# Block sums of the down projection's weights: made in attention with two tiles instead of beside the SSD with six

## The chip, the core and the metric

The kernel runs on one core of one Trainium2 chip. The metric is the device time of one execution in microseconds (us); the time of a kernel is the median of several runs. The engines of the core work side by side, each through its own list of instructions in order: TensorE (PE in the profile, with its weight loads as PEld), VectorE (DVE), ScalarE (ACT), GpSimd (POOL), and SyncE (SP), which here issues nearly all DMAs. Tiles lie in SBUF, matmul results in PSUM.

## What is computed

One decoder block over 1024 tokens of 1024 channels: a Mamba-2 SSD and a differential attention side by side, merged by gates, then a gated convolutional FFN. Cut to what matters here:

```python
h = rms_norm(x, pre_norm1_w[layer]) * (1.0 + sc1) + sh1
z, xbc, dt_raw, q, k, v, gates = jnp.split(h @ w_in[layer], IN_SPLITS, axis=-1)
y_ssd = ssd_branch(z, xbc, dt_raw, ...)
y_att = diff_attention_branch(q, k, v, ...)      # softmax 1 minus lam times softmax 2, per head
merged = gate_ssd * (y_ssd @ w_ssd_o[layer]) + gate_att * (y_att @ w_attn_o[layer])
x = x + g1 * rms_norm(merged @ w_out[layer], post_norm1_w[layer])
h2 = rms_norm(x, pre_norm2_w[layer]) * (1.0 + sc2) + sh2
u = causal_dwconv(h2 @ w_up[layer], conv_ffn_w[layer], conv_ffn_b[layer])
f = (jax.nn.gelu(u_gate, approximate=True) * u_val) @ w_down[layer]
x = x + g2 * rms_norm(f, post_norm2_w[layer])
```

## The kernel before

Every large matmul is split by hand: each operand is held as a rounded high part and a low part (the remainder), and three products replace one. On top of that, the up and the down projection use Strassen's scheme (in Winograd's form) on two by two blocks: seven block products instead of eight, for which sums and differences of the blocks of the weights are needed.

For the down projection these are the *block sums* of this document. `w_down` is 2816 x 1024. Its rows are taken as two halves of eleven groups (`KF` = 11) of 128 rows, its columns as two halves of 512, so group k has four blocks b11, b12, b21, b22 of 128 x 512. Needed are t1 = b12 - b11, t2 = b22 - t1, t3 = b22 - b12 and t4 = b21 - t2. They do not depend on the input, are made early in the kernel, written to the DRAM tensors `wtd["12"]` and `wtd["34"]`, and read back in the down projection at the end (`right_part`, L2161).

The kernel goes through these stages, by their place in the profiled execution (us from the start of its span): the norm and the projections of x up to 1147; the **SSD** from 1147 to 1744; the q and k projections' first blocks and the SSD's output projection up to about 2270; **attention** from about 2270 to 3300; the attention's output projection, `w_out`, the up projection from about 3640 to 4900, and the down projection.

*The SSD* (L1186 to L1242) goes through 16 units u, each half of a chunk of 128 tokens. In a unit are called, in the order in which they are written: `chunk_in(u+1)` (transposes and small products, the scaled input `xd` on DVE, `xdd` on GpSimd), `fill(2)`, `chunk_decay(u+1)` (decay matrices `M`, on ScalarE), `chunk_mask(u+1)` on DVE, `chunk_out(u)` (products `po` and `py`, then `tt` and `yt` on DVE), and `chunk_state(u)` (product `pst`, then `prev` on DVE). `fill(n)` emits n steps of the projection that makes the values v, six matmuls with 512 columns for two steps, which keeps TensorE at work. `run_bg(n)` runs n small pieces of a queue of background work, here mostly the chunk's norm. The list of engines given to `manual_schedule` (L1186: TensorE, VectorE, ScalarE, SP) says whose order is the one written; an engine that is not named is ordered by a planner with its own estimates. `sum_dn(u, n)` (L1180) is called at four places in a unit (L1212, L1215, L1223, L1227) and takes the next piece of `all_sums`, one subtraction of 128 x 512 on DVE. Sums are made in units 0 to 11, except unit 7 and half of unit 8. Six tiles of 512 KB serve them: four (`wdr`) for the blocks of two groups, which are loaded two groups ahead, and two (`wds`) for results, which are stored two by two.

*Attention* (L1592 to L1658) goes through 64 items t = (head j, block i of 128 queries). While item t is finished, the scores of t+1 are made. In the order of the code: `scores(t+1)` puts the score products on TensorE and behind them the transposes of item t's probabilities; then, on DVE, the mask (L1465 or L1475) and the row maxima (L1466 or L1476). `fill` emits steps of a stream of projections (three matmuls with 512 columns each), about four steps in an item. `probs(t+1)` has the exponentials on ScalarE (L1478, L1486, L1489), and on DVE the reciprocal (L1492), a coefficient (L1493) and the combination of the two softmaxes `p` (L1494). Then come `values(t)` on TensorE and at the end the bookkeeping. Background pieces are taken at four places in an item, two of them between the exponentials and the reciprocal. An item with i below 4 has up to 512 keys and uses one score buffer of two; one with i of 4 or more uses both. `load_heads` (L1425) loads the next head's queries, keys and values after item i = 3 (4 for the first head). The manual list here (L1592) is TensorE, VectorE, ScalarE and GpSimd, so SP's order comes from the planner.

Tiles of 512 KB come from `Slots` (L36), a pool of 43 with a first-in, first-out free list: what is freed first is taken first.

Of the kernel before, what the change touches and what calls it, by code (L numbers as in the profile page):

```python
# [11 lines left out]
F32 = mybir.dt.float32  # L12
F32R = mybir.dt.float32r
AF = mybir.ActivationFunctionType
ALU = mybir.AluOpType
AX = mybir.AxisListType

P = 128
D = 1024
S = 1024  # L20
HALF = 512
# [41 lines left out]
def kernel(ctx: ExitStack, tc: tile.TileContext, a: dict, out: bass.AP, dbg=None):  # L63
    nc = tc.nc
    V, A, G, T, SP = nc.vector, nc.scalar, nc.gpsimd, nc.tensor, nc.sync
# [6 lines left out]
    SL = Slots(sp, NSLOT)  # L72
# [331 lines left out]
    b12 = [hT[k][1] for k in range(KH)]  # L404
# [22 lines left out]
    KF = NFF // 2  # L427
    gld = {n: dp.tile([P, KF, HALF], F32, tag=f"gld_{n}", name=f"gld_{n}") for n in ("a11", "a12", "a22")}
    gld |= {n: dp.tile([P, KF, 2, HALF], F32, tag=f"gld_{n}", name=f"gld_{n}") for n in ("s12", "s34")}
    wtd = {n: dp.tile([P, KF, 2, HALF], F32, tag=f"wtd_{n}", name=f"wtd_{n}") for n in ("12", "34")}  # L430
# [170 lines left out]
    with tc.manual_schedule(engines={EN.PE, EN.DVE, EN.Activation, EN.SP}):  # L601
# [97 lines left out]
        for m, (kind, *_) in enumerate(pairs):  # L699
            last = m == len(pairs) - 1  # L700
            cg, cv = cgv[m % 2]
            x_, z_ = (0, 2) if m % 2 else (1, 3)
# [75 lines left out]

    dn_ops = deque()

    def down_load(k):
        if k < KF:
            for i in range(2):
                r0 = (k + KF * i) * P
                SP.dma_start(wdr[k % 2][i].rearrange("p h c -> p (h c)"), a["w_down"][r0 : r0 + P, :])

    def down_sums(k):
        (b11, b12), (b21, b22) = [(t[:, 0, :], t[:, 1, :]) for t in wdr[k % 2]]
        t1, t2, t3, t4 = wds[0][:, 0, :], wds[0][:, 1, :], wds[1][:, 0, :], wds[1][:, 1, :]
        V.tensor_tensor(t1, b12, b11, op=ALU.subtract)  # L790
        yield
        V.tensor_tensor(t2, b22, t1, op=ALU.subtract)
        SP.dma_start(wtd["12"][:, k, :, :], wds[0])
        yield
        V.tensor_tensor(t3, b22, b12, op=ALU.subtract)
        yield
        V.tensor_tensor(t4, b21, t2, op=ALU.subtract)
        SP.dma_start(wtd["34"][:, k, :, :], wds[1])
        down_load(k + 2)
        yield  # L800

    def all_sums():
        for k in range(KF):
            yield from down_sums(k)


    sm1 = SL.get("sm1", F32, (P, 8, 8, NH))
# [14 lines left out]
    f = lambda t: t.rearrange("p c h -> p (c h)")  # L822
# [350 lines left out]
            SP.dma_start(seq_w[n].rearrange("p k c -> p (k c)"), a[kind][b])  # L1173

    load_z(0)
    wdr = [[SL.get(f"wdr{i}{j}", F32, (P, 2, HALF)) for j in range(2)] for i in range(2)]
    wds = [SL.get(f"wds{i}", F32, (P, 2, HALF)) for i in range(2)]
    sums_dn = all_sums()

    def sum_dn(u, n):  # L1180
        if u == 7 or (u == 8 and n < 2):
            return
        for _ in range(2 if u < 2 and n == 3 else 1):
            next(sums_dn, None)

    with tc.manual_schedule(engines={EN.PE, EN.DVE, EN.Activation, EN.SP}):  # L1186
        for k in range(2):
            down_load(k)
        chunk_in(0)
        fill(2)  # L1190
        chunk_decay(0)
        chunk_mask(0, 0)
        chunk_mask(0, 1)
        lamt = const("lamt", [P, 2, 64])
        lams = const("lams", [P, 2])
        nlam = const("nlam", [P, 1])
        rl = rows[:, R_LAM : R_LAM + 256].rearrange("p (a b d) -> p a b d", a=2, b=2)
        V.tensor_tensor(lamt, rl[:, :, 0, :], rl[:, :, 1, :], op=ALU.mult)
        V.reduce_sum(lams, lamt, axis=AX.X)
        A.activation(lams, lams, AF.Exp)  # L1200
        V.tensor_tensor(nlam, lams[:, 1:2], lams[:, 0:1], op=ALU.subtract)
        V.tensor_scalar(nlam, nlam, -LAM_INIT, None, op0=ALU.add)
        subw = const("subw", [P, 1])
        V.tensor_scalar(subw, vec[:, V_SUB : V_SUB + 1], 1.0 - LAM_INIT, None, op0=ALU.mult)
        fill(4)
        for u in range(16):
            nxt = u + 1 < 16
            if nxt:
                chunk_in(u + 1)
            fill(2)  # L1210
            run_bg(2)
            sum_dn(u, 0)  # L1212
            if nxt:
                chunk_decay(u + 1)
            run_bg(1)  # L1215
            sum_dn(u, 1)
            if nxt:
                chunk_mask(u + 1, 0)
            fill(2)
            chunk_out(u, (lambda: chunk_mask(u + 1, 1)) if nxt else (lambda: None))  # L1220
            fill(3)
            run_bg(3)
            sum_dn(u, 2)  # L1223
            chunk_state(u)
            fill(1 if u % 3 else 0)
            run_bg(1)
            sum_dn(u, 3)  # L1227
            if u % 2 == 1:
                chunk_norm(u // 2)
            if u == 11:  # L1230
                assert next(sums_dn, None) is None
                SL.put(*wdr[0], *wdr[1], *wds)
                yr = [SL.get(f"yr{i}") for i in range(4)]
                ropc, rops = SL.get("ropc"), SL.get("rops")
                SP.dma_start(ropc, a["ropc"])
                SP.dma_start(rops, a["rops"])
                fetch_seq(0)
                fetch_seq(1)
            elif u == 12:
                load_y(0)  # L1240
        fill(16 * KD)
        run_bg(len(bg))  # L1242
# [345 lines left out]
    nfill = sum(2 * KD for _ in blocks) - NFIRST - NLAST  # L1588
    share = [4, 4, 4, 3, 4, 4, 4, 4]
    load_heads(0)  # L1590
    done = 0
    with tc.manual_schedule(engines={EN.PE, EN.DVE, EN.Activation, EN.Pool}):  # L1592
        for _ in range(NFIRST - 6):
# [5 lines left out]
        for t, (j, i) in enumerate(items):  # L1599
            quota = (j * sum(share) + sum(share[: i + 1])) * nfill // (8 * sum(share)) - done  # L1600
            done += quota
            quota += 2 if t == len(items) - 2 else 0
            f1 = quota // 2
            nxt = t + 1 < len(items)
            x = {}

            def first_turn():
                x[0] = transposes(t, 0)

            if nxt:  # L1610
                sc = scores(t + 1, first_turn)
            else:
                first_turn()
            fill(f1)
            f2 = (quota - f1 + 1) // 2
            if i >= 4:
                x[4] = transposes(t, 4)
            if nxt:
                probs(t + 1, sc, 2)
            run_bg(1)  # L1620
            values(t, 0, *x[0])
            fill(f2)
            if i % 4 == 2 and pend is not None:
                out_o(*pend)
            if i >= 4:
                values(t, 4, *x[4])
            fill(quota - f1 - f2)
            run_bg(1)
            emitted["values"] += 1
            if t == 55:  # L1630
                SL.put(*thl[0], *thl[1], *qst[0], *kst[0], *klo[0], vt[0])
                stg = [SL.get(f"stg{i}", F32, (P, 2, HALF)) for i in range(2)]
                for _ in range(4):
                    att_in()
            elif t > 56:
                for _ in range(2 if i % 2 else 1):
                    if n_att < 10:
                        att_split()
            if j < 7 and i == (4 if j == 0 else 3):
                load_heads(j + 1)  # L1640
            if i % 4 == 3:
                norm_o(j, i // 4)
                pend = (j, i // 4)
            elif i % 4 == 2:
                pend = None
# [775 lines left out]
```

## Time and profile before

| | us |
|---|---|
| timed runs | 1841.74, 1842.9, 1843.09 |
| median of the timed runs | 1842.9 |
| profiled execution, span from its first to its last instruction | 5463.1 |
| TensorE busy in the profiled execution | 5447.4 |
| VectorE busy | 1312.2 |
| ScalarE busy | 898.9 |
| GpSimd busy | 139.0 |

The profiled execution has no time of its own beside its span. The span is three times as long as a timed run; durations that are taken from the profile must be read with that in mind, TensorE's above all.

The profile lists for each engine how long it was busy, groups of instructions by line of the code (a group's row: line, engine, operation, output<-inputs, shapes, count | busy us, mean ns of one | idle time of the engine ahead of them and what ended it), the waits of one engine for another, the DMAs, and a timeline. In a row of stretches stand, for each engine, the busy us and, after it in brackets, the number of instructions.

### The profile page before, as it was taken

What the parts mean: (1) busy time and instruction counts of PE and PEld (TensorE: products, weight loads), DVE (VectorE), ACT (ScalarE), POOL (GpSimd) and SP (SyncE); (2) the same over time, 40 slices, a digit from 0 to 9 for tenths busy, and PEclk for the clock granted to TensorE, in tenths of its full rate; (3) what the DMA queues carried; (4) which work ended last, traced back from release to release, by engine and by line L of the source; (5) the groups of instructions that cost most, each with busy time, mean ns of one, the idle gap of its engine ahead of it and who ended that gap; (6) DMA issues with size and microseconds to landing.
All of it is one profiled execution on the core that took longest, in us unless ns stands there. A gap on an engine that the chain in (4) does not pass through costs nothing.

```text
span 5463.1 us, 24362 instructions
## 1 busy us (share of the span) xinstructions
PE 5447.4 (100%) x8922; PEld 3303.6 (60%) x8922; DVE 1312.2 (24%) x1984; ACT 898.9 (16%) x1744; POOL 139.0 (3%) x128
## 2 busy tenths in 40 slices
PE   9999999999999999999999999999999999999999
PEld 4555557766665555566677776556555555555555
DVE  4122222222221200022222231212333333332211
ACT  3111110011111100011122221102212111121210
POOL 0000000001110000000000000000000000000000
DMA  4021012212111212121122112210011111123221
GB/s 165 31 77 46 29 35 72 70 64 100 64 67 46 54 35 81 35 52 47 48 72 69 56 47 95 81 46 31 31 44 39 44 35 41 40 71 116 87 63 60
DMA packets 131368, 326.22 MB, mean 60 GB/s; under 512 B 14881, under 2 KB 39089, under 8 KB 131250
## 3 DMA queue, kind: packets, MB, share of 16 engines
q1 hardware_dynamic: 130290, 321.53, 18.2%
q0 software_dynamic: 960, 3.15, 0.2%
q8 instruction: 70, 1.15, 0.1%
q14 instruction: 48, 0.39, 0.0%
HBM read 229.45 MB, written 95.17 MB: 59 GB/s over the span
## 4 chain that ended last, share of the span: by engine, by line
PE 100%; issue 0%; ACT 0%; POOL 0%; DVE 0%; DMA 0%; DVEq 0%; POOLq 0%; ACTq 0%
PE upx L1822 4%; PE upx L1823 4%; PE upx L1821 4%; PE o L1515 4%; PE v L1028 2%; PE z L116 2%; PE v L1029 2%; PE z L118 2%; PE z L117 2%; PE xx L534 2%; PE so L117 2%; PE so L118 2%; PE xx L532 2%; PE upy L1821 2%; PE upy L1822 2%; PE upy L1823 2%
## 5 line engine op out<-in xcount | busy, mean ns | idle before, releaser
L1515 PEld LDWEIGHTS o<-vt,aT 128*128 128x128 f32 x576 | 201.1, 415 | 39.5 <-issue 33.8
L1821 PE MATMUL upx<-t,wu_t 128*128 128x512 f32 x264 | 218.9, 829 | 0.0
L1823 PE MATMUL upx<-t,wu_t 128*128 128x512 f32 x264 | 218.7, 828 | 0.0
L1822 PE MATMUL upx<-t,wu_t 128*128 128x512 f32 x264 | 218.7, 828 | 0.0
L1515 PE MATMUL o<-vt,aT 128*128 128x128 f32 x576 | 214.2, 578 | 0.0
L1456 PE MATMUL sc<-kst,qst 128*128 128x512 f32 (+2 forms) x192 | 141.7, 742 | 0.0
L1457 PE MATMUL sc<-klo,qst 128*128 128x512 f32 (+2 forms) x192 | 141.4, 746 | 0.0
L118 PE MATMUL so<-yT,w_ssd_o_lo 128*128 128x512 f32 x128 | 140.8, 1100 | 0.0
L117 PE MATMUL so<-yT,w_ssd_o_hi 128*128 128x512 f32 x128 | 140.8, 1100 | 0.0
L116 PE MATMUL so<-yT,w_ssd_o_hi 128*128 128x512 f32 x128 | 139.3, 1088 | 0.0
L1503 ACT COPY aT<-at 128x512 f32<-128x512 f32 (+2 forms) x96 | 45.9, 479 | 562.2 <-PE at L1502 562.2
L1822 PEld LDWEIGHTS upx<-t,wu_t 128*128 128x128 f32 x264 | 93.5, 354 | 63.8 <-issue 63.8
L1821 PEld LDWEIGHTS upx<-t,wu_t 128*128 128x128 f32 x264 | 93.4, 354 | 63.7 <-issue 62.7
L1823 PEld LDWEIGHTS upx<-t,wu_t 128*128 128x128 f32 x264 | 92.3, 350 | 63.8 <-issue 63.8
L1114 PEld LDWEIGHTS py<-xd,M 128*128 128x128 f32 x256 | 107.1, 596 | 34.8 <-issue 34.8
L1028 PE MATMUL v<-wv_hi,hT 128*128 128x512 f32 x96 | 121.5, 1266 | 0.0
L116 PE MATMUL z<-wz_hi,hT 128*128 128x346 f32 (+1 forms) x144 | 121.1, 841 | 0.0
L118 PE MATMUL z<-wz_hi,hT 128*128 128x346 f32 (+1 forms) x144 | 119.7, 832 | 0.0
L117 PE MATMUL z<-wz_lo,hT 128*128 128x346 f32 (+1 forms) x144 | 119.1, 827 | 0.0
L1502 PE MATMUL at<-ident,p 128*128 128x128 f32 x288 | 117.1, 576 | 0.0
L2184 PE MATMUL dx<-wdt_hi,g_hi 128*128 128x512 f32 x132 | 109.5, 830 | 0.0
L2186 PE MATMUL dx<-wdt_hi,g_lo 128*128 128x512 f32 x132 | 109.2, 827 | 0.0
(553 smaller groups left out, 10212.8 us busy)
## 6 DMA issues: line engine op xcount, KB each, us to landing
adas<-in_w_ada SPq DMA_DIRECT2D x32, 512.0 KB, 3.9
wdr<-in_w_down SPq DMA_DIRECT2D x22, 512.0 KB, 5.5
wtd<-wds SPq DMA_DIRECT2D x22, 512.0 KB, 2.9
wuf<-in_w_up SPq DMA_DIRECT2D x22, 512.0 KB, 3.5
gld_s<-gsum SPq DMA_DIRECT2D x22, 512.0 KB, 2.6
gst<-gld_s SPq DMA_DIRECT2D x20, 512.0 KB, 4.3
wdt_raw<-wtd SPq DMA_DIRECT2D x20, 512.0 KB, 3.9
wuv<-in_w_up SPq DMA_DIRECT2D x19, 512.0 KB, 3.6
```

The costliest lines, as they stand in the source:

```text
L116: T.matmul(ps, lh, rh, start=(i == 0), stop=False)
L117: T.matmul(ps, lh, rl, start=False, stop=False)
L118: T.matmul(ps, ll, rh, start=False, stop=(i == n - 1))
L1028: T.matmul(ps, xh_, wh, start=(k == 0), stop=False)
L1456: T.matmul(sc[:, n0:n1], qs_[s][:, tsl], ks_[s][:, n0:n1], start=True, stop=False)
L1457: T.matmul(sc[:, n0:n1], qs_[s][:, tsl], kl[s][:, n0:n1], start=False, stop=True)
L1502: T.transpose(ptr[:, k * P : (k + 1) * P], pt_[i % 2][0][:, (k0 + k) * P : (k0 + k + 1) * P], ident)
L1515: T.matmul(po_of[j, grp][:, qi, :], at[:, k, :], vt[j % 2][:, kt, :], start=(kt == 0), stop=(kt == i))
L1821: T.matmul(out_, wh, xh_, start=(k == 0 and first), stop=False, skip_group_check=not first)
L1822: T.matmul(out_, wh, xl_, start=False, stop=False, skip_group_check=not first)
L1823: T.matmul(out_, wl, xh_, start=False, stop=(k == end), skip_group_check=not first)
L2184: T.matmul(o, gh[:, kk, tsl], wh, start=(k == 0 and not more), stop=False, skip_group_check=more)
```

## The change

The same 44 subtractions are made, on the same engine. In the SSD all of them go, with their loads, their stores and the six tiles. In attention two tiles are taken, `wdr[0]` for b11 and b12 and `wdr[1]` for b21 and b22. A group takes five items: in the first four, one subtraction each, in place, in this order: b11 becomes t1 = b12 - b11, b12 becomes t3 = b22 - b12, b22 becomes t2 = b22 - t1, b21 becomes t4 = b21 - t2. Each result is stored at once, as 256 KB, and each tile is loaded for the next group behind the subtraction after which nothing needs its blocks any more: `wdr[0]` in the third item, `wdr[1]` in the fourth. The fifth item has none. Eleven groups in five items each make the items t = 0 to 54. The subtraction stands at the end of an item, ahead of the next item's scores and mask. After item 55 the tiles are freed with those of the attention.

```diff
-    def down_load(k):
+    def down_load(k, i):
         if k < KF:
-            for i in range(2):
-                r0 = (k + KF * i) * P
-                SP.dma_start(wdr[k % 2][i].rearrange("p h c -> p (h c)"), a["w_down"][r0 : r0 + P, :])
-
-    def down_sums(k):
-        (b11, b12), (b21, b22) = [(t[:, 0, :], t[:, 1, :]) for t in wdr[k % 2]]
-        t1, t2, t3, t4 = wds[0][:, 0, :], wds[0][:, 1, :], wds[1][:, 0, :], wds[1][:, 1, :]
-        V.tensor_tensor(t1, b12, b11, op=ALU.subtract)
-        yield
-        V.tensor_tensor(t2, b22, t1, op=ALU.subtract)
-        SP.dma_start(wtd["12"][:, k, :, :], wds[0])
-        yield
-        V.tensor_tensor(t3, b22, b12, op=ALU.subtract)
-        yield
-        V.tensor_tensor(t4, b21, t2, op=ALU.subtract)
-        SP.dma_start(wtd["34"][:, k, :, :], wds[1])
-        down_load(k + 2)
-        yield
+            r0 = (k + KF * i) * P
+            SP.dma_start(wdr[i].rearrange("p h c -> p (h c)"), a["w_down"][r0 : r0 + P, :])
 
     def all_sums():
+        (b11, b12), (b21, b22) = [(t[:, 0, :], t[:, 1, :]) for t in wdr]
         for k in range(KF):
-            yield from down_sums(k)
+            for n, (o, x_, y_) in enumerate(((b11, b12, b11), (b12, b22, b12), (b22, b22, b11), (b21, b21, b22))):
+                V.tensor_tensor(o, x_, y_, op=ALU.subtract)
+                SP.dma_start(wtd[("12", "34", "12", "34")[n]][:, k, n // 2, :], o)
+                if n > 1:
+                    down_load(k + 1, n - 2)
+                yield
+            yield
...
-    wdr = [[SL.get(f"wdr{i}{j}", F32, (P, 2, HALF)) for j in range(2)] for i in range(2)]
-    wds = [SL.get(f"wds{i}", F32, (P, 2, HALF)) for i in range(2)]
-    sums_dn = all_sums()
...
-            sum_dn(u, 0)
...
-            sum_dn(u, 1)
...
-            sum_dn(u, 2)
...
-            sum_dn(u, 3)
...
     load_heads(0)
+    wdr = [SL.get(f"wdr{i}", F32, (P, 2, HALF)) for i in range(2)]
+    sums_dn = all_sums()
+    for i in range(2):
+        down_load(0, i)
...
             emitted["values"] += 1
+            if t < 55:
+                next(sums_dn, None)
             if t == 55:
+                assert next(sums_dn, None) is None
+                SL.put(*wdr)
```

More of the change, by code (lines that the diff above doesn't have):

```diff
@@ L1175 @@
     load_z(0)
-    wdr = [[SL.get(f"wdr{i}{j}", F32, (P, 2, HALF)) for j in range(2)] for i in range(2)]
-    wds = [SL.get(f"wds{i}", F32, (P, 2, HALF)) for i in range(2)]
-    sums_dn = all_sums()
[L1180 to L1184, printed above, removed]
     with tc.manual_schedule(engines={EN.PE, EN.DVE, EN.Activation, EN.SP}):
-        for k in range(2):
-            down_load(k)
         chunk_in(0)
@@ L1230 @@
             if u == 11:
-                assert next(sums_dn, None) is None
-                SL.put(*wdr[0], *wdr[1], *wds)
                 yr = [SL.get(f"yr{i}") for i in range(4)]
```

## The prediction

> **What bounds the kernel now.** I read the head of the page first, because it says which engine fills the span.
>
> ```profile
> span 5463.1 us, 24362 instructions
> PE 5447.4 (100%) x8922; PEld 3303.6 (60%) x8922; DVE 1312.2 (24%) x1984; ACT 898.9 (16%) x1744; POOL 139.0 (3%) x128
> ```
>
> TensorE fills the profiled execution, but that execution lasted 5463.1 us and the timed ones 1842.9 us. So its matmuls ran slower than in the timed runs, and what hides behind them in the profile need not hide there. How much slower comes from the starts of consecutive matmuls with 512 moving columns, in the timeline, TensorE alone, in the SSD and in attention.
>
> ```profile
> 1318.71 1.16 PE L1029 MATMUL v<-wv_lo,hT 128*128 128x512 f32 x1
> 1319.55 1.16 PE L1030 MATMUL v<-wv_hi,hT 128*128 128x512 f32 x1
> ```
>
> ```profile
> 2680.15 1.16 PE L1411 MATMUL gap<-hT,ga_hi 128*128 128x512 f32 x1
> 2680.99 0.94 PE L1412 MATMUL gap<-hT,ga_lo 128*128 128x512 f32 x1
> ...
> 2683.36 0.91 PE L1412 MATMUL gap<-hT,ga_lo 128*128 128x512 f32 x1
> 2683.97 0.92 PE L1456 MATMUL sc<-kst,qst 128*128 128x512 f32 x1
> ```
>
> One matmul starts 0.84 us after the other up to about 2682 us, and 0.61 to 0.62 us after it from there on: I use 0.84 and 0.62. Counted in such steps the span is 2682/0.84 + 2781/0.62 = 7680 steps. The page has 15.7 us in which TensorE is idle (5463.1 - 5447.4), so a step in the timed runs takes at most (1842.9 - 15.7)/7680 = 0.238 us. It must be shorter, since the timed runs also hold the waits that a quicker TensorE uncovers; with some 60 us for those of the two stages below and of all the others it is (1842.9 - 76)/7680 = **0.23 us**, which is an estimate. A stretch of the trace is then multiplied by 0.23/0.84 = 0.274 before 2682 us and by 0.23/0.62 = 0.371 behind it, while VectorE (DVE), ScalarE (ACT), GpSimd (POOL) and the DMAs keep the durations of their rows.
>
> The Trainium skill bears on this step: "TensorE: Matmul & The Clock Gate", section "Wait — 56ns, not 53.3ns?", has 215.7 ns from start to start at 512 columns once the clock is free. The traced 0.62 and 0.84 us disagree, the bound of 0.238 does not. By it the sum below would end near 1848 us instead of 1850, with more given back in the SSD and more lost in attention.
>
> Next the busy times by stretch: the SSD units that carry sums (1167 to 1607 us), then attention's items 0 to 55 on either side of the change of pace. Columns: PE, PEld, DVE, ACT, POOL, clock (no throttle is recorded), DMA share, GB/s.
>
> ```profile
> 1167.00:1607.00 440.00, 440.00 (x682) 275.05 (x681) 104.09 (x146) 67.46 (x180) 67.15 (x50) 1.00 0.22 77
> 2282.00:2664.00 382.00, 382.00 (x626) 247.42 (x625) 79.93 (x162) 64.20 (x172) 4.03 (x4) 1.00 0.18 47
> 2664.00:3175.00 511.00, 511.00 (x1169) 363.44 (x1168) 141.55 (x286) 121.19 (x323) 9.06 (x9) 1.00 0.22 63
> ```
>
> At 0.23 us a step the SSD stretch needs 440 x 0.274 = 121 us of TensorE, with 104 us of DVE and 67 us of POOL beside it. Attention needs about 290 us, with 221 us of DVE. So TensorE is the bound of both stages only by a little, and a subtraction is hidden only where an item leaves room for it.
>
> **What is removed from the SSD.** 44 subtractions on DVE, and on SP 22 loads and 22 stores of 512 KB, all in units u = 0 to 11.
>
> ```profile
> L795 DVE TENSOR_TENSOR wds<-wdr,wdr 128x512 f32<-128x512 f32 x11 | 10.9, 989 | 0.0
> L792 DVE TENSOR_TENSOR wds<-wdr,wds 128x512 f32<-128x512 f32 x11 | 9.7, 884 | 0.2
> L797 DVE TENSOR_TENSOR wds<-wdr,wds 128x512 f32<-128x512 f32 x11 | 9.2, 836 | 0.0
> L790 DVE TENSOR_TENSOR wds<-wdr 128x512 f32<-128x512 f32 x11 | 8.4, 760 | 0.0
> L1116 DVE TENSOR_TENSOR yt<-py,yt 128x512 f32<-128x512 f32 x12 | 8.3, 692 | 63.5 <-PE py L1114 43.8 <-issue 19.7
> L1130 DVE TENSOR_TENSOR prev<-pst,prev 128x512 f32<-128x512 f32 x10 | 6.9, 692 | 95.6 <-PE pst L1128 95.6
> L1111 DVE TENSOR_TENSOR tt<-po,sm 128x512 f32<-128x512 f32 x10 | 6.9, 691 | 57.8 <-PE po L1110 57.8
> L1079 DVE TENSOR_TENSOR sm<-px,tri 128x128 f32<-128x128 f32 x11 | 3.2, 291 | 54.1 <-ACT sm L1078 54.1
> ```
>
> The four lines of sums take 38.2 us. The same shape takes 684 to 989 ns, and the timeline shows why:
>
> ```profile
> 1310.11 1.89 POOL L1082 TENSOR_TENSOR xdd<-xd,sm 128x512 f32<-128x512 f32 x1 [0.69 <-DVE xd L1080]
> ...
> 1311.02 1.53 DVE L795 TENSOR_TENSOR wds<-wdr,wdr 128x512 f32<-128x512 f32 x1
> ...
> 1312.47 0.68 DVE L797 TENSOR_TENSOR wds<-wdr,wds 128x512 f32<-128x512 f32 x1
> ```
>
> A subtraction alone takes 0.68 us; one that starts under a GpSimd instruction takes 1.53, as if it waited the 0.85 us until that one is over. So DVE operations with both inputs in SBUF and GpSimd's take turns. Per unit (a twelfth of the stretch) DVE has 104.09/12 = 8.7 us and POOL 5.6; only DVE's four groups that read PSUM, 25.3/12 = 2.1 us, can run beside GpSimd. In turns the unit needs up to 8.7 + 5.6 - 2.1 = 12.2 us, and without the waits that its rows already hold (8.1 us of the sums alone, 38.2 - 44 x 0.684, and more of GpSimd's) down to 10; I take 11, the middle. TensorE needs 36.7 x 0.274 = 10.0. A unit is too long by 0 to 2.2 us, taken as 1.0; over the 11 units that have four sums that makes 11 us, of which 2 pass in the room that the order leaves, since `pst` needs `tt` only a few matmuls later. Without the sums (2.7 us a unit) the turns take 8.3 us and TensorE's 10.0 hides them. **Given back: 9 us**, bounds 0 and 24. The freed DMA time (23 MB) is worth nothing there, since no wait of the stage ends on it.
>
> **What attention gets.** 44 subtractions on DVE, one in each of four items out of five for t = 0 to 54, with 44 stores of 256 KB and 22 loads of 512 KB on SP. GpSimd has only 13 us of work in this stage, so a subtraction takes 0.684 us: 30.1 us of DVE in all. It stands behind the combination `p` of item t+1 and ahead of the mask of t+2. DVE is in order: behind it wait the mask, the maxima, ScalarE's exponentials, the combination, and on TensorE the transposes of `p`. One head (j = 5), cut at its eight reciprocals (L1492):
>
> ```profile
> 2951.90:2963.80 11.90, 11.90 (x30) 9.08 (x30) 2.56 (x7) 2.41 (x9) 0.00 (x0) 1.00 0.02 4
> 2963.80:2972.80 9.00, 9.00 (x20) 6.08 (x19) 3.44 (x11) 2.78 (x14) 1.01 (x1) 1.00 0.44 113
> 2972.80:2986.00 13.20, 13.20 (x28) 8.86 (x27) 3.84 (x8) 3.39 (x8) 0.00 (x0) 1.00 0.04 15
> 2986.00:2998.80 12.80, 12.80 (x34) 9.31 (x33) 3.40 (x8) 2.83 (x6) 0.00 (x0) 1.00 0.54 143
> 2998.80:3014.30 15.50, 15.50 (x38) 11.13 (x37) 3.76 (x8) 3.74 (x9) 0.00 (x0) 1.00 0.22 44
> 3014.30:3030.40 16.10, 16.10 (x38) 10.89 (x38) 5.40 (x13) 4.16 (x15) 1.01 (x1) 1.00 0.24 77
> 3030.40:3048.10 17.70, 17.70 (x42) 12.08 (x41) 5.74 (x9) 4.83 (x9) 0.00 (x0) 1.00 0.26 75
> 3048.10:3063.70 15.60, 15.60 (x43) 12.15 (x43) 2.53 (x5) 2.56 (x7) 0.00 (x0) 1.00 0.48 134
> ```
>
> TensorE's need (first column x 0.371) is 4.4, 3.3, 4.9, 4.7, 5.8, 6.0, 6.6 and 5.8 us. DVE's turn is its busy time and the part of the exponential that no background piece fills:
>
> ```profile
> L1489 ACT ACTIVATION_READ_ACCUMULATOR p<-sc,nmx 128x1 f32 x56 | 11.2, 201 | 0.0
> L1486 ACT ACTIVATE p<-sc,nmx 128x1024 f32<-128x1024 f32 x7 | 7.8, 1119 | 0.0
> ```
>
> The longest is 1.12 + 0.20 us; I take half, 0.7. The turns are 3.3, 4.1, 4.5, 4.1, 4.5, 6.1, 6.4 and 3.2 us, the room 1.1, -0.8, 0.4, 0.6, 1.3, -0.1, 0.2 and 2.6. A further 0.684 costs 0, 0.68, 0.28, 0.08, 0, 0.68, 0.48 and 0 = 2.2 us, and since a late item starts the next one late, the third and seventh cost all of it: 2.8. Times 4/5 (items with a subtraction) and 55/8 (items through eight) that is 15 us; the first heads, which split more (L1391), have less room, so I take **16 us lost**. Bounds: 0 if every item has room, 30.1 if none has. A gain is excluded, since work is only added.
>
> The transfers: a load waits on SP for the stores out of its tile, and behind it stand stores and the next head's loads.
>
> ```profile
> wdr<-in_w_down SPq DMA_DIRECT2D x22, 512.0 KB, 5.5
> wtd<-wds SPq DMA_DIRECT2D x22, 512.0 KB, 2.9
> ```
>
> Store and load land within 2.9 + 5.5 = 8.4 us, and the tile is read again three items later, about 3 x 5.2 us. So I cost it at 0, and up to 30 us if a transfer is late in each of the ten reloads. Halving the stores' runs has no row; they are off DVE's way, and I take 0.
>
> **The sum.** In the profiled execution both stages lie under a TensorE that is busy throughout, so its span stays at 5463 us within a few. In the timed runs: 1842.9 - 9 + 16 = **1850 us**.
>
> **The rivals.** (1) Faster. The items have room for every subtraction, and the SSD gives back 16 (1.5 us a unit): 1827 us. For it speaks how long DVE waits in attention for the scores:
>
> ```profile
> DVE sc L1475 <- PE sc L1457: 207.3, 56, 12.8
> DVE sc L1465 <- PE sc L1457: 195.1, 27, 14.0
> ```
>
> That is 402 us for 30 us of work. Against it: it is the slow TensorE's wait. It decides where a subtraction fits between `p` and the next scores, 0.684 us of room, in the heavy items too. Chance 0.24. (2) No change, 1843 us: TensorE hides both ends in the timed runs as in the profile. The Trainium skill, "Perfetto Trace Analysis", section "Identifying the Most-Contended Engine", says to judge by the engine of highest occupancy, for TensorE by its weight loads; the page has 60% there against DVE's 24%, so by that rule this change moves nothing. Against it stand the eight windows. Chance 0.15. (3) Much slower: the reload of a tile comes late behind the next head's loads (the DMA share is up to 0.54 in one window, at a third of the timed pace), and DVE waits 2.5 us in each of ten reloads: 1875 us. Chance 0.13. It decides once a load lands later than three items. That the change did not do what it says is no case: DVE's order is written out in both places.
>
> **How the numbers follow.** The forecast has 0.48. Slower by over 0.2%, which is about what a measurement of this kernel can tell from no change, are the forecast and (3): 0.61; faster (1): 0.24; within 0.2% (2): 0.15. The range 1826 to 1876 us reaches to (1) and (3) and leaves the outer bounds out.
>
> **What would show it.** In the profile after: subtractions of 0.68 us between 2282 and 3175 us with none of 1.53; 38 us less DVE in the SSD, and shorter L1080 and L1082 there; a span within a few us of 5463. An idle DVE ahead of a subtraction that a load ends speaks for (3). A timed run below 1839 shows the step on attention's room wrong, one above 1867 shows the transfers or the carried lateness undersized.

## The result and the profile after

| | us |
|---|---|
| before, median of 4 runs | 1842.93 (1841.74 to 1843.09) |
| after, median of 4 runs | 1853.74 (1851.88 to 1858.09) |
| ratio | 1.0062, 95% interval 1.0051 to 1.0074 |
| profiled execution after, span | 1850.1 |

The change makes the kernel slower by 10.8 us, where 7 were forecast. The head of the page of the kernel after, to be read against the two lines of before that open the prediction:

```profile
span 1850.1 us, 24399 instructions
PE 1819.0 (98%) x8922; PEld 1521.2 (82%) x8922; DVE 1287.6 (70%) x1984; ACT 894.1 (48%) x1744; POOL 135.6 (7%) x128
```

This execution ran at the pace of the timed ones (its own time was 1851.88 us). So the profile of before, three times as long, was one odd execution and not a property of the profiler. The unchanged kernel before was therefore profiled once more (`before_again` below, span 1840.7 us), and the rest of the comparison is made with that profile. The timeline of TensorE in the kernel after, in the SSD, shows the step between matmuls of 512 columns:

```profile
421.36 0.40 PE L1020 MATMUL v<-wv_lo,hT 128*128 128x512 f32 x1
421.59 0.39 PE L1021 MATMUL v<-wv_hi,hT 128*128 128x512 f32 x1
421.82 0.39 PE L1019 MATMUL v<-wv_hi,hT 128*128 128x512 f32 x1
```

The step is 0.23 us. Next the busy times by stretch: units 0 to 11 of the SSD, to within 2 us, and attention; columns as in the prediction. First the kernel before, profiled again, then the kernel after:

```profile
340.00:466.00 126.00, 125.93 (x702) 102.28 (x700) 115.17 (x156) 71.90 (x195) 71.14 (x51) 1.00 0.76 270
646.00:1000.00 354.00, 351.35 (x2047) 301.25 (x2046) 247.68 (x514) 209.84 (x567) 15.12 (x15) 1.00 0.54 154
```

```profile
340.00:466.00 126.00, 126.00 (x701) 102.48 (x700) 80.50 (x113) 71.53 (x194) 62.48 (x51) 1.00 0.33 108
646.00:1000.00 354.00, 345.08 (x1995) 293.70 (x1994) 263.78 (x544) 205.56 (x556) 18.79 (x15) 1.00 0.73 213
```

In the SSD VectorE lost 35 us of work and TensorE did the same work in the same time: it was busy throughout before, and it is busy throughout after. From the first to the last product of `xbcT` with itself (tile `px`; L1075, after the change L1066) the SSD took 151.1 us before (337.2 to 488.3) and takes 150.8 after (336.7 to 487.5). In the stretch of attention TensorE had 2.65 us of idle time before and has 8.92 after. The score products (tile `sc`) give the length of attention, by their first and last start; the fourth and fifth numbers are these, first before, then after:

```profile
L1457 PEld LDWEIGHTS sc<-klo,qst x192: 187/188/192, 652.8 to 996.5; 128*128 128x128 f32 x192
```

```profile
L1430 PEld LDWEIGHTS sc<-klo,qst x192: 186/188/192, 652.1 to 1005.3; 128*128 128x128 f32 x192
```

Attention starts 0.7 us earlier and lasts 353.2 instead of 343.7 us, 9.5 longer. What lies behind it keeps its length (844.8 us from there to the end against 844.2). The whole difference is made in attention, and the SSD gave back 0.3 us. Two of the subtractions' rows before, and both after, in minimum, median and maximum of ns:

```profile
L790 DVE TENSOR_TENSOR wds<-wdr x11: 677/682/1702, 347.7 to 461.0; 128x512 f32<-128x512 f32 x11
L795 DVE TENSOR_TENSOR wds<-wdr,wdr x11: 675/686/1527, 351.6 to 465.8; 128x512 f32<-128x512 f32 x11
```

```profile
L790 DVE TENSOR_TENSOR wdr<-wdr x22: 681/684/692, 661.7 to 960.0; 128x512 f32<-128x512 f32 x22
L790 DVE TENSOR_TENSOR wdr<-wdr,wdr x22: 682/684/694, 666.1 to 953.3; 128x512 f32<-128x512 f32 x22
```

Before, 18 of the 44 took longer than 0.7 us, up to 1.7, and each of these 18 overlaps a GpSimd instruction in the trace; in attention all take 0.68.

### The profile page after: what moved, and what is told of

The parts are those of the page before. It is cut to its first block, busy times and chain, and to the rows that moved or that the text cites. A ratio compares the mean times of both kernels' runs of the same rounds, so it can differ in the third digit from the quotient of the medians.

```text
span 1850.1 us, 24399 instructions
## 1 busy us (share of the span) xinstructions
PE 1819.0 (98%) x8922; PEld 1521.2 (82%) x8922; DVE 1287.6 (70%) x1984; ACT 894.1 (48%) x1744; POOL 135.6 (7%) x128
## 4 chain that ended last, share of the span: by engine, by line
PE 74%; DVE 12%; ACT 6%; DMA 3%; issue 3%; SPq 1%; POOL 1%; DVEq 0%; POOLq 0%; ACTq 0%
PE upx L1803 4%; PE upx L1804 4%; PE upx L1802 4%; PE upy L1803 2%; PE upy L1802 2%; PE upy L1804 2%; PE dx L2166 2%; PE dx L2167 2%; PE v L1019 2%; PE dx L2165 2%; PE z L117 2%; PE z L118 2%; PE z L116 2%; PE dy L2167 2%; PE dy L2166 2%
## 5 line engine op out<-in xcount | busy, mean ns | idle before, releaser
L1802 PE MATMUL upx<-t,wu_t 128*128 128x512 f32 x264 | 103.1, 391 | 0.5 <-DVE cv L2230 0.4
L1803 PE MATMUL upx<-t,wu_t 128*128 128x512 f32 x264 | 102.8, 389 | 0.2 <-DVE t L1920 0.2
L1804 PE MATMUL upx<-t,wu_t 128*128 128x512 f32 x264 | 102.7, 389 | 0.0
L1488 PEld LDWEIGHTS o<-vt,aT 128*128 128x128 f32 x576 | 74.9, 191 | 10.6 <-ACT aT L1476 6.3
L1488 PE MATMUL o<-vt,aT 128*128 128x128 f32 x576 | 81.2, 277 | 0.8 <-ACT aT L1476 0.4
L94 ACT ACTIVATE g_hi<-gst 128x1024 fp32r<-128x1024 f32 (+1 forms) x42 | 41.5, 989 | 67.2 <-DMA gst<-gld_s 36.1
L1449 DVE TENSOR_REDUCE nmx<-sc 128x1 f32<-128x640 f32 (+3 forms) x64 | 65.6, 1025 | 2.2
L1430 PE MATMUL sc<-klo,qst 128*128 128x512 f32 (+2 forms) x192 | 63.3, 346 | 1.4 <-DMA klo<-kld 1.4
L1429 PE MATMUL sc<-kst,qst 128*128 128x512 f32 (+2 forms) x192 | 63.9, 341 | 0.0
L1820 DVE SCALAR_TENSOR_TENSOR ug<-cg,vec,ug 128x1023 f32<-128x1023 f32 (+1 forms) x44 | 56.3, 1281 | 6.1 <-ACT ug L1819 5.3
L1802 PEld LDWEIGHTS upx<-t,wu_t 128*128 128x128 f32 x264 | 49.6, 188 | 11.7 <-DVE cv L2230 1.4
L1803 PEld LDWEIGHTS upx<-t,wu_t 128*128 128x128 f32 x264 | 49.6, 188 | 10.6 <-DVE t L1920 0.5
L1804 PEld LDWEIGHTS upx<-t,wu_t 128*128 128x128 f32 x264 | 49.6, 188 | 10.3
L1475 PE MATMUL at<-ident,p 128*128 128x128 f32 x288 | 47.8, 275 | 7.2 <-DVE p L1467 7.0
L2165 PE MATMUL dx<-wdt_hi,g_hi 128*128 128x512 f32 x132 | 51.3, 389 | 0.0
```

The costliest lines, as they stand in the source:

```text
L1429: T.matmul(sc[:, n0:n1], qs_[s][:, tsl], ks_[s][:, n0:n1], start=True, stop=False)
L1430: T.matmul(sc[:, n0:n1], qs_[s][:, tsl], kl[s][:, n0:n1], start=False, stop=True)
L1449: V.reduce_max(nmx[:, bq, s : s + 1], sc[:, :L], axis=AX.X, negate=True)
L1488: T.matmul(po_of[j, grp][:, qi, :], at[:, k, :], vt[j % 2][:, kt, :], start=(kt == 0), stop=(kt == i))
L1802: T.matmul(out_, wh, xh_, start=(k == 0 and first), stop=False, skip_group_check=not first)
L1803: T.matmul(out_, wh, xl_, start=False, stop=False, skip_group_check=not first)
```

## The experiments

Two theories were stood against each other first. **Room**: the SSD hid the sums almost wholly, and an item of attention has no room for a subtraction at its end, where TensorE waits for the next `p`. **Transfers**: the stores and reloads on SP's queue cost the time. Times are medians; the ratio is to the kernel before, run on the same chip beside each. The four kernels named `only_...` ran on another chip than the rest of the experiments; the kernel before took 1842.4 to 1842.6 us on both.

### The kernel before, and no sums at all

`before_again` is the kernel before, unchanged.

> The kernel before, unchanged, for a profile at the pace of the timed runs. Every theory expects 1843 us within 0.2%. If its matmuls with 512 columns start 0.227 us apart, as in the profile of the changed kernel, the two profiles can be laid side by side stage by stage. The prediction's steps expect the SSD about 9 us longer than in the changed kernel and attention about 16 to 20 us shorter.

1842.92 us, ratio 1.0002 (0.9993 to 1.0012), with a profiled span of 1840.7 us: the long execution did not come back.

`none` is the kernel after with the sums taken out:

```diff
-    for i in range(2):
-        down_load(0, i)
...
-            if t < 55:
-                next(sums_dn, None)
...
-            raw = wp.tile([P, 2, HALF], F32, tag="wraw", name=f"wd{n}_{kp}_raw", bufs=3)
...
-            SP.dma_start(raw[:, :nk], wtd[("12", "34")[i // 2]][:, 2 * kp : 2 * kp + nk, i % 2, :])
+            return load_moving(a["w_down"], i // 2 * KF + 2 * kp, nk, i % 2 * HALF, HALF, f"wd{n}_{kp}")
```

> No block sums anywhere: the subtractions, their loads and their stores are left out, and the down projection reads blocks of w_down of the same size in their place. Theory A (both stages pay for the subtractions on DVE: some 9 us in the SSD before, some 16 to 20 us in attention after) expects 1834 us, 9 below the kernel before. Rival B (the SSD paid nothing, the whole difference of 11 us is attention's price) expects 1843.

1841.64 us, ratio 0.9995 (0.9986 to 1.0004). The sums beside the SSD cost 1.3 us in all, no more than the measurement can tell from nothing; theory A's 1834 us, and with it the 9 us given back, falls. VectorE's waits of more than 1 us in total, in the same stretch of the SSD, show what they had lain in (us in total, times, longest); first before, then without sums:

```profile
DVE prev L1130 <- PE pst L1128: 3.8, 5, 1.6
DVE sm L1079 <- ACT sm L1078: 1.9, 4, 1.1
DVE yt L1147 <- POOL ssy L139: 1.8, 3, 0.6
DVE M L1103 <- ACT M L1098: 1.3, 2, 1.0
```

```profile
DVE prev L1121 <- PE pst L1119: 18.1, 9, 2.2
DVE M L1094 <- ACT M L1089: 18.0, 17, 2.4
DVE sm L1070 <- ACT sm L1069: 9.6, 6, 3.6
```

Without sums VectorE waits 46 us there, with them 9: the sums stood in waits and filled them nearly to the brim.

### How full the SSD was

`before_twice` makes each of the 44 subtractions of the kernel before a second time, right behind the first, with the same result:

```diff
         V.tensor_tensor(t1, b12, b11, op=ALU.subtract)
+        V.tensor_tensor(t1, b12, b11, op=ALU.subtract)
```

> The kernel before with each of its 44 subtractions beside the SSD made twice, 30 us more of DVE there. If DVE was at its brim there (8 to 10 us of idle time left in the 126 us with sums) as the turns with GpSimd say, it is 15 to 25 us slower, about 1862 us. If the SSD had much room for them, 1843 to 1848 us.

1866.62 us, ratio 1.0130 (1.0116 to 1.0145): 24 us more for 44 x 0.684 = 30 us of VectorE. TensorE's waits in the SSD, which before had no entry in this list:

```profile
PE pst L1132 <- DVE tt L1115: 18.1, 6, 6.0
```

Not all of the 24 us is VectorE's work, though. The same twelve units, cut at the first `px` of the second and of the fourteenth unit, before and with the sums made twice, and in the latter the 4 us behind the end of the longest wait (the number behind GpSimd's is the granted clock):

```profile
342.50:467.00 124.50, 124.43 (x694) 100.84 (x693) 113.64 (x154) 69.43 (x188) 70.71 (x50) 1.00 0.77 275
341.40:490.90 149.50, 131.39 (x693) 104.00 (x692) 146.24 (x196) 69.71 (x189) 75.39 (x50) 0.94 0.64 229
```

```profile
376.00:380.00 4.00, 4.00 (x14) 2.53 (x15) 3.96 (x7) 0.06 (x1) 2.98 (x3) 0.63 1.00 332
```

TensorE waits for 18 us, and its matmuls take 7 us longer (131.39 against 124.43), in stretches in which the granted clock is below 1.00. So the room that was left beside the first sums was about 12 us (30 - 18), which agrees with the 10.9 us in which VectorE was idle there before (124.50 - 113.64): about one microsecond a unit. That they were hidden was a close thing, but hidden they were.

### The transfers without the subtractions, and the subtractions in another place

`after_no_sub` leaves the 44 subtractions out (stores and loads stay):

```diff
-                V.tensor_tensor(o, x_, y_, op=ALU.subtract)
```

> The changed kernel without its 44 subtractions; the loads and stores stay, so that the raw blocks are stored. Theory A (DVE's order pays) expects the time of the kernel with no sums at all, about 1834 us, within 3 us. Rival C (the transfers pay: the DMAs or SP's queue hold attention up) expects that the time stays near 1850.

1845.19 us (1841.95 to 1846.83), ratio 1.0011 (1.0002 to 1.0020): 8.5 us below the kernel after, 3.6 above `none`. Neither theory's number came: the larger part of attention's price is the subtractions', a smaller one the transfers'.

`after_gap` has every subtraction, between the exponentials and the reciprocal of the next item, where VectorE waits for ScalarE:

```diff
-    def probs(t, sc, n_bg):
+    def probs(t, sc, n_bg, with_sum=False):
...
+        if with_sum:
+            next(sums_dn, None)
...
-            if t < 55:
-                next(sums_dn, None)
```

> The changed kernel with the subtraction put elsewhere in the item: ahead of the background pieces, between the exponentials and the reciprocal, where DVE waits for ScalarE. Theory A, with room as the price: the exponential's wait of up to 1.3 us takes part of the 0.68 us, and half of the loss in attention goes, about 1844 us. Rival D (what counts is DVE's whole work in an item, wherever it stands) expects 1853 as before; if the background pieces fill that wait already, it is no better either.

1845.22 us (1842.80 to 1846.98), ratio 1.0014 (1.0005 to 1.0023). With all the work and all the transfers, it costs what the transfers alone cost. It is the better place, but not better than the kernel before, and none of these could be by much: `none`, which does no sums at all, is only 1.3 us below it.

### Half of the subtractions, and an eighth of the bytes

`subs_light` keeps the 22 subtractions that fall into items i = 2, 3, 6, 7, `subs_heavy` those in i = 0, 1, 4, 5; the transfers stay, and the other 22 results are left out:

```diff
-                V.tensor_tensor(o, x_, y_, op=ALU.subtract)
+                if at_item[0] in (2, 3, 6, 7):
+                    V.tensor_tensor(o, x_, y_, op=ALU.subtract)
...
+                at_item[0] = i
```

> The changed kernel with its loads and stores, but of the 44 subtractions only the 22 that fall into items i = 2, 3, 6 and 7; in the other items the block is stored as it is. By the prediction's table of room, the stretches behind these items have 0.6, 1.3, 2.6 and 1.1 us to spare. Theory A (a subtraction costs what its item's room doesn't take) expects 1845 to 1846 us, that is nothing beside the kernel without subtractions (1845.2). Rival D (each of the 44 costs the same fifth of a microsecond, 8.5/44) expects 1849.5.

> The other half: only the 22 subtractions in items i = 0, 1, 4 and 5 are made, whose stretches had -0.8, 0.4, -0.1 and 0.2 us to spare by the prediction's table. Theory A expects nearly the whole price, 1852 to 1853 us. Rival D expects 1849.5.

1846.64 us (1843.51 to 1849.28), ratio 1.0021 (1.0011 to 1.0030), and 1847.68 us (1846.89 to 1850.84), ratio 1.0030 (1.0018 to 1.0041). Both lie between none and all of the subtractions, but the runs scatter by 4 to 6 us and the two can't be told apart. The 1852 us that theory A expected of the heavy half was not reached by any run, and the halves are 1.5 and 2.5 us above `after_no_sub`, together less than half of the 8.5 us of all 44.

`no_sub_small` has no subtractions, moves 16 of the 128 partitions in each load and store, and reads `w_down` in the down projection as `none` does:

```diff
-            SP.dma_start(wdr[i].rearrange("p h c -> p (h c)"), a["w_down"][r0 : r0 + P, :])
+            SP.dma_start(wdr[i][:16].rearrange("p h c -> p (h c)"), a["w_down"][r0 : r0 + 16, :])
...
-                SP.dma_start(wtd[("12", "34", "12", "34")[n]][:, k, n // 2, :], o)
+                SP.dma_start(wtd[("12", "34", "12", "34")[n]][:16, k, n // 2, :], o[:16])
```

> The changed kernel without subtractions, with every load and store still issued by SP in its place, but of 16 partitions where there were 128, an eighth of the bytes; the down projection reads blocks of w_down instead. The kernel with whole transfers took 1845.2 us, the one without any 1841.6. Theory E (the bytes pay: attention's own transfers come later because the DMAs are busier) expects 1842. Rival F (SP's queue pays: it waits for stores and subtractions ahead of the next head's loads) expects 1845.

1843.24 us (1841.62 to 1846.37), ratio 1.0004 (0.9995 to 1.0013): between `none` and `after_no_sub`, told from neither by its interval. Its profile says more than its time. Where the third head passes to the fourth, a product with the keys' low part waits; the waits of TensorE in attention of this kernel:

```profile
PE at L1474 <- DVE p L1466: 2.5, 9, 0.5
PE sc L1429 <- DMA klo<-kld: 1.4, 1, 1.4
```

SP's queue shows why. The loads of `klo` for the fourth head in the timeline of SP, in `none` and in this kernel:

```profile
745.17 1.25 SPq L1224 DMA_DIRECT2D klo<-kld x2
...
765.06 1.15 SPq L1224 DMA_DIRECT2D klo<-kld x2
```

```profile
766.49 1.23 SPq L1223 DMA_DIRECT2D klo<-kld x2
767.83 0.53 SPq L1220 DMA_DIRECT2D qst<-qd x1
768.40 1.08 SPq L1223 DMA_DIRECT2D kst<-khd x2
771.04 1.50 SPq L1223 DMA_DIRECT2D klo<-kld x2
```

Both profiles have the item at the same time (the third head's first reciprocal, which comes 24 us earlier, is at 741.2 and at 740.9 us), but with the sums' stores and reloads on SP the first pair is issued 21 us later and the last pair 6 us later, at 771. The four land after (from issue; minimum, median, maximum; again `none` first):

```profile
DMA to landing us min/median/max: 4.0/4.3/4.6
```

```profile
DMA to landing us min/median/max: 8.0/9.1/10.2
```

The product that needs the last one, due at about 781 (40 us behind that reciprocal, as in `none`), waits. Neither the late issue nor the long landing would have made it wait alone: issued at 772.1 and landed in 4.6 us, or issued at 765.6 and landed in 10.2, the load would have been there in time. The bytes are an eighth, and the wait is the one of the full transfers: for this wait it is SP's order, in which all the loads of the head now stand close behind each other, and not the amount. Whether the amount pays for the rest of the time the run doesn't say.

### The subtractions without the transfers

To have VectorE's price free of that scatter, four kernels load the two tiles once and subtract in them over and over: no stores, no reloads, and the down projection reads `w_down`.

```diff
-                SP.dma_start(wtd[("12", "34", "12", "34")[n]][:, k, n // 2, :], o)
-                if n > 1:
-                    down_load(k + 1, n - 2)
```

Beside that, `only_all` has the subtractions where the change has them, `only_light` and `only_heavy` have the halves as above, and `only_gap` has all of them in the exponentials' wait.

> Left out: the stores of the results and all loads of the two tiles but the first, so the 44 subtractions work over and over on the same two tiles, and the down projection reads the blocks of w_down in place of the sums. The subtractions stand at the end of the items, as in the changed kernel. It stands beside the kernel without any sums (1841.6 us). Theory A (an item has no room for a subtraction behind the combination p, whatever the transfers do): the whole difference of 8.5 us between the changed kernel and the one without its subtractions is there, 1850.1 us. Rival B (the subtractions cost that much only because a reload or a store stands ahead of them, in their tiles): 1842 to 1844 us.

> As the kernel with all 44 subtractions and one load of the two tiles, but with the 22 alone that fall into items i = 2, 3, 6 and 7. Theory A, each item by itself: the spacing of the reciprocals in these items grew by 4.8 us in seven heads of the changed kernel's profile, of 9.4 in all, so about half of the 8.5 us, 1845.9 us. Rival C (lateness is carried: one late item makes the next one late, and with free items in between it is made good): 1.5 us, as the earlier pair of halves measured beside the transfers, 1843.1 us.

> As the kernel with all 44 subtractions and one load of the two tiles, but with the 22 alone that fall into items i = 0, 1, 4 and 5. Theory A, each item by itself: 4.6 of 9.4 us of the spacing of the reciprocals, 1845.8 us, and together with the other half the 8.5 us of all 44. Rival C (lateness is carried): 2.5 us, 1844.1 us, and the two halves together at most 5 us, clearly less than all 44.

> As the kernel with all 44 subtractions and one load of the two tiles, but each subtraction stands between the exponentials and the reciprocal, ahead of the background pieces there, and not at the end of the item. Theory A (the place decides: VectorE waits there for ScalarE, and the subtraction lies in that wait): 1841.6 to 1842.6 us, and the 3.6 us by which the changed kernel with the subtraction moved there was over the kernel without sums are the transfers'. Rival D (a subtraction costs its time wherever it stands, and the earlier kernel was quicker for another reason): as with the subtractions at the end, about 1850 us.

| | us | ratio to before | over `none` |
|---|---|---|---|
| only_all | 1849.86 (1849.32 to 1850.21) | 1.0039 (1.0025 to 1.0053) | 8.2 |
| only_light | 1843.97 (1843.06 to 1845.56) | 1.0009 (1.0001 to 1.0018) | 2.3 |
| only_heavy | 1846.39 (1845.85 to 1847.20) | 1.0021 (1.0012 to 1.0030) | 4.8 |
| only_gap | 1842.52 (1841.85 to 1843.50) | 1.0000 (0.9991 to 1.0009) | 0.9 |

This settles the place. The same 30 us of VectorE cost 8.2 us at the end of an item and 0.9, no more than can be told from nothing, in the wait ahead of the reciprocal; rival D falls, and B with it. Why, from TensorE's and VectorE's waits in attention, in `none`, `only_all` and `only_gap`:

```profile
PE at L1475 <- DVE p L1467: 2.2, 8, 0.5
```

```profile
PE at L1472 <- DVE p L1464: 7.0, 18, 0.9
```

```profile
PE at L1474 <- DVE p L1466: 2.5, 8, 0.6
```

```profile
DVE rsm L1465 <- ACT p L1462: 35.2, 30, 3.1
DVE rsm L1465 <- ACT p L1459: 26.6, 28, 1.8
```

```profile
DVE rsm L1464 <- ACT p L1459: 25.5, 23, 2.7
DVE rsm L1464 <- ACT p L1456: 16.4, 23, 1.8
```

The last two fences are VectorE's wait for the exponentials, in `none` and in `only_gap`: 62 us without subtractions, 42 with them there, so about 20 of their 30 us lie in it. At the end of an item a subtraction makes the next item late: the mask, the maxima, the exponentials and the combination `p` all shift, and the transposes (`at`) wait for `p` in 18 places instead of 8. The trace lists 4.8 us of such waits more in `only_all`; the rest of the 8.2 us it doesn't list by a releaser.

The halves are less clear. Together they make 7.1 us, where independent items would give 8.2 and rival C at most 5. The light half's 2.3 us is nearer to C's 1.5 than to A's 4.3, the heavy half's 4.8 is over both numbers, and a sum of two medians is not certain to a microsecond. The profiles say more, each taken in one execution. Attention, from the first to the last weight load of `sc<-klo`, takes 343.8 us in `none`, 352.1 in `only_all`, 345.4 in `only_light`, 348.6 in `only_heavy` and 344.4 in `only_gap`. By the starts of the reciprocals, the stretches that the light half's subtractions make late grow by 3.2 us in all and the others shrink by 1.5; with the heavy half it is 6.4 and 1.6. So the price is paid item by item, 9.6 us in the two halves together, and a part of it is made good where the next item has no subtraction. With all 44 only one item in five is free, and 8.3 us stay.

### What the transfers cost

Five pairs differ in the transfers alone (the down projection's source aside): after over only_all 3.9 us, after_no_sub over none 3.6, after_gap over only_gap 2.7, subs_light over only_light 2.7, subs_heavy over only_heavy 1.3. No single pair is certain, but all five have one sign. In the profiles they are told by the landing of `klo` between 700 and 870 us (from issue, minimum, median and maximum), in `only_all` and in the kernel after:

```profile
DMA to landing us min/median/max: 3.8/5.8/6.9
```

```profile
DMA to landing us min/median/max: 4.2/7.5/9.5
```

and by TensorE's wait for it in the kernel after, which `none` and the four kernels of this last group don't have:

```profile
PE sc L1430 <- DMA klo<-kld: 1.4, 1, 1.4
```

By the starts of the reciprocals the third head, up to the fourth's first one, takes 0.9 to 1.5 us longer in every kernel that has the transfers than in the same kernel without them; in the profile of `after_no_sub` this 1.3 us is all by which attention's items are longer than in `none`. A second place changes from profile to profile. In `after_gap` three subtractions wait for their own reloads, the mechanism of the prediction's third rival:

```profile
DVE wdr L790 <- DMA wdr<-in_w_down: 6.2, 3, 4.9
```

The kernel after has no such wait in its profile, which is its quickest run. Its timed runs spread over 6 us and those of `only_all` over 1. That loads come late in some executions and not in others would fit this, but no trace shows it, so that stays open.

## Why the prediction was right, and where it was not

The sign and the size came out: 1853.74 us lies in 1826 to 1876, 3.7 above the forecast. But two terms were too large and one was left at nothing: -9 + 16 + 0 was forecast, and about -1 + 8 + 4 was measured. The two large errors, 8 us each, cancelled; that the sum came so near is luck.

**TensorE's step of 0.23 us** was right. The Trainium skill, "TensorE: Matmul & The Clock Gate", section "Wait — 56ns, not 53.3ns?", has 215.7 ns; the rows above have 230, so the measurement decides. By the page's figure the sum was 1848 us, further off.

**The span of 5463 us that was to stay** was wrong: 1850.1. The step treated an execution that didn't recur as what a profile of this kernel looks like.

**"A unit is too long by 0 to 2.2 us, taken as 1.0"** failed; the bound 0 was the truth, nearly. Two numbers were off. TensorE's need of a unit is 10.35 us, not 10.0: cut at the first `px` of the second and of the fourteenth unit, twelve units take 446.8 us in the first profile (1161.4 to 1608.2), where the prediction took a stretch of 440, and 124.2 in the profile after (342.1 to 466.3), a factor of 0.278 and not 0.274. That alone would have left 5 of the 9 us (0.65 in 11 units, less 2). And the turns of VectorE and GpSimd were not 11: VectorE's 115.17 and GpSimd's 71.14 us went into 126, so at least 60 us of the one lay beside the other, 5 us a unit, where 2.1 were allowed beside the waits that the rows hold. The prediction took the middle between the bounds without a row that spoke for it. (The "11 units that have four sums" are 44/4: in the code units 0 to 6 and 9 to 11 have four or five, unit 8 has two and unit 7 none.) `before_twice` shows that the direction of the thought was sound: about one microsecond more a unit, and the stage would have been VectorE's.

**"16 us lost"** in attention was 8.2 (`only_all` over `none`). The mechanism was the one named, what waits behind a subtraction between `p` and the next mask. The duration of 0.684 us was right. The size failed at TensorE's need. The same head j = 5, cut at the same eight reciprocals, in `none`:

```profile
872.90:877.60 4.70, 4.70 (x29) 4.14 (x29) 2.57 (x7) 2.43 (x8) 0.00 (x0) 1.00 0.63 145
877.60:881.80 4.20, 4.20 (x23) 3.63 (x23) 3.37 (x11) 2.77 (x14) 1.01 (x1) 1.00 0.89 229
881.80:886.60 4.80, 4.80 (x29) 4.06 (x28) 3.83 (x7) 3.50 (x8) 0.00 (x0) 1.00 0.17 65
886.60:891.60 5.00, 4.96 (x32) 4.10 (x31) 3.29 (x7) 2.87 (x8) 0.00 (x0) 1.00 0.65 190
891.60:897.60 6.00, 6.00 (x38) 5.21 (x36) 3.71 (x8) 3.52 (x9) 0.00 (x0) 1.00 1.02 210
897.60:903.80 6.20, 6.20 (x39) 5.41 (x37) 5.17 (x13) 4.01 (x15) 1.01 (x1) 1.00 0.67 226
903.80:910.90 7.10, 7.10 (x45) 6.13 (x44) 5.59 (x9) 4.66 (x9) 0.00 (x0) 1.00 0.58 165
910.90:916.60 5.70, 5.52 (x38) 4.90 (x38) 2.53 (x5) 2.57 (x7) 0.00 (x0) 1.00 1.01 304
```

They add up to 43.7 us, where the multiplied rows gave 41.5. The factor 0.371 was the ratio of the steps of two matmuls with 512 columns at their closest. Over all of attention's matmuls the mean step went from 511/1169 = 0.437 us in the prediction's row to 351.35/2047 = 0.172, a factor of 0.39, 6% more. With the lengths of these rows and the prediction's own 0.7 us of unfilled wait, the room is 1.4, 0.1, 0.3, 1.0, 1.6, 0.3, 0.8 and 2.5 us. A subtraction then costs 0.55, 0.41 and 0.35 in the second, third and sixth stretch and nothing elsewhere, 1.31 x 4/5 x 55/8 = 7.2 us for the stage, beside the 8.2 measured; the prediction's carried lateness, a quarter more, would make it 9. A small error of the need becomes a large one of the loss, since the room is a difference of two nearly equal numbers. That this one number explains the size is worked out, not tried by itself, and the places bear it out only in part. By the reciprocals of `none` and `only_all` the second and third stretches of the heads grew by 4.9 us in all, where this working gives 5.3; the sixth grew by 0.6, where it gives 1.9; and the others, where it gives nothing, by 2.8.

**The transfers at 0** were about 3 us, 1.3 to 3.9 by the pairs. The step compared a tile's landing with the time until it is read again. In the profile after that went wrong nowhere; what went wrong is the loads that stand behind on SP, the next head's keys, named there and priced at nothing. The 1.4 us wait is shown; the rest of the 3 us is not put to a place.

**The first rival** (room in every item) is wrong in what it gives back and in the place. The wait for the scores that it leaned on shrinks from 402 us to 19 at the timed pace (16.2 and 2.6 in `before_again`); another one, the 62 us for the exponentials ahead of the reciprocal, hides nearly all of the work when the subtraction is put there. **The second** (TensorE hides both ends) holds for the SSD and fails in attention; the rule of the Trainium skill, "Perfetto Trace Analysis", section "Identifying the Most-Contended Engine", picks TensorE here rightly (82% of weight loads to VectorE's 70% in the profile after). What an added 30 us of VectorE costs was decided by their place in its order all the same. **The third** was right in that loads come late behind others, but in the kernel after it is the head's loads that are late and not the reload, and 25 us above the forecast's 1850 was too large by a factor of about eight. **Signs in the profile:** subtractions of 0.68 us throughout, as said. VectorE's relief in the SSD was 35 us in the stretch, near the 38 said. In the mean of that stretch L1082 got shorter (1590 to 1476 ns), but L1080 did not (1011 to 1063), so that sign failed.

## What to carry to other kernels

Before work is moved from one stage to another, ask of both ends not how busy the engine is but what stands behind the new instruction in its queue: 30 us of VectorE cost 8 at one place in a loop and 1 a few instructions earlier, in a wait that was there anyway. If the profile ran at another pace than the timed runs, a scaled length can be off by 5%, as here, and a loss that is the difference of two nearly equal times can come out double. And count a moved transfer by what is queued behind its issue, not by its bytes alone.

## What was not expected of the hardware

One profiled execution of a kernel took 5463.1 us where its timed runs took 1842.9, with the granted clock at 1.00 in every stretch that was read; matmuls of 512 columns started 0.84 and then 0.62 us apart. The same kernel again, the kernel after and the other experiments had spans of 1839.9 to 1865.0 us. No run here shows what caused it.

In `before_twice` the granted clock fell with TensorE's longer waits: about the end of those of 5.97, 3.43 and 3.55 us and behind it, it was 0.50 to 0.85 in rows of 4 us; about those of 2.74, 1.40 and 1.01 us it stayed at 1.00. The matmuls of the stretch took 7 us longer in all, so such a wait cost more than its length. Where between 2.74 and 3.43 us the limit lies, and whether it is the length alone that counts, these six waits don't say.

VectorE's subtractions with both inputs in SBUF and GpSimd's instructions delay each other at the timed pace as well: 0.68 us alone, 1.53 and up to 1.70 beside GpSimd, whose busy time in the stretch was 71.14 us with the sums and 62.48 without. Even so their rows overlap by at least 5 us a unit; how much of that is the waiting that the rows hold, and how much is work side by side, no run here separates.
